# A hybrid attention and recurrence layer: head pairs projected earlier, half of an output projection inside the last pair, query swaps on GpSimd

## The chip, the cores and the metric

The kernel runs on one core of a Trainium2 chip. The metric is the device time of one execution in microseconds (us). Its engines are TensorE (PE; PEld are its weight loads), VectorE (DVE), ScalarE (ACT), GpSimd (POOL) and SyncE (SP), whose queue issues all DMA transfers of this kernel. TensorE's clock is granted at 2.4 or at 1.2 GHz; the profile gives the mean grant of a stretch as a share of the higher one.

## The reference, cut to what matters

One layer on 1024 frames of width 1024, with 16 learned frames in front (L = 1040):

```
u    = rms_norm(h);  proj = u @ w_in
       -> fq, fk, fv (8 heads x 64), ff (8), hq, hf, hi, hg (4 heads x 128)
fox  = per head: softmax(q.k/8 + c_t - c_s, causal) @ v,  c = cumsum(log_sigmoid(ff + bias))
hgrn = S_t = diag(f_t) S_{t-1} + k_t v_t^T,  o_t = S_t^T q_t;  rms_norm(o) * silu(hg)
h    = h + concat(fox, hgrn) @ w_out
h    = h + (silu(u2 @ w_gate) * (u2 @ w_up)) @ w_down,   u2 = rms_norm(h)
out  = rms_norm(h)[16:]
```

All is float32. The kernel splits each operand of a product into a high and a low part and forms three products (`mm3`: high x high, high x low, low x high), so that every product of the formulas is three on TensorE. A split is a cast on ScalarE (high part, L135) and a subtraction on VectorE or GpSimd (low part, L136).

## The kernel before, in words

The stages, in the order of the program: norm and transposition of the input (u, high and low, in `uT`); the recurrence heads (`hgrn_proj`, `hgrn_compute`), the values of the attention heads (`fox_v`) and their gates between them; the attention by pairs of heads (`fox_proj`, `fox_compute`); the output projection by tiles of 128 frames (`out_proj`) with the second norm; the FFN, in 22 blocks, by a scheme that saves products; the last product with `w_ffn_down` and the final norm. The change touches the attention and the start of the output projection, from about 345 to 600 us of the span.

**Projection of a pair** (`fox_proj`, L488). Weights for the keys and the queries of two heads are loaded and split (`load_m`; from pair 1 on GpSimd makes the low part, w_lo). `keys(i)` forms a third of the 1040 keys, `queries(i)` a half of the 1024 queries, each with 24 products into one of three `dense` PSUM banks; ScalarE evacuates the high part and VectorE the low part, into KS (keys) and QA (queries) of each head: one head dimension of 64 partitions holds the high part, the other 64 the low part. KS and QA come from pool `fxk0` for pairs 0 and 2, `fxk1` for 1 and 3, one buffer each: a pair can write them once the pair before last is done. `keys(0)` and `queries(0)` are traced before the pair's attention; `keys(1)` behind its group 0; `keys(2)` and `queries(1)` behind its group 1 (`rest`).

**Attention of a pair** (`fox_compute`, L604) runs over 4 groups g of 256 queries, and in each over its 2 heads (`fox_group`, L529). Group g needs keys up to 16 + 256(g + 1) and queries 256g to 256(g + 1). QB holds the same queries as QA with the halves of 64 partitions swapped; it is made by two transfers within SBUF (L532, L533). The scores are QA x KS and QB x KS (L546, L547) in PSUM bank `g`; VectorE adds the gate sums nl (or the masked block dm that GpSimd makes of them, L540) and takes the minimum (L552); ScalarE forms the exponential (L557); TensorE transposes it (L577), ScalarE and VectorE split it into PH and PL (L581, L582), TensorE multiplies it with v (L587), and the result goes through `mixp` to `mix_dram` (L598, L599, L616, L617). At the start of a pair `fox_head_load` loads v and nl (a row of 1040 broadcast to 128 partitions) and VectorE takes 4 columns of nl as tg (L524); GpSimd shifts nl by tg after each group (L602). v and nl have one buffer for each of the two heads, QB two.

**Output projection.** `out_proj(t)` (L687) loads the 8 blocks of `mix_dram` for its tile in three parts (4 to 7 are the recurrence heads, 0 to 3 the attention pairs), splits them into mh and ml (one buffer each), and forms 8 x 3 products for each half of 512 columns, the last pair's block at the end. Its weights are w_out in 8 blocks, cast and split into `woh` and `wol` by `load_wo` (L651): four blocks behind group 1 of pair 3, four behind its group 2, into space that is free once u is no longer read (`uT_pool` closes in `after_group(1)`).

**What sets the order.** The program is traced in the order of the Python code, and the framework's planner then sets the order on each engine: going through modelled time, it gives each engine, of the instructions whose inputs and buffers it takes to be ready, the one traced first. Each engine and SyncE's queue then keep that order on the chip and wait in it. So an instruction that is traced later can be run earlier, where an engine would have nothing else to do.

Of the kernel before, what the change touches and what calls it, by code (L numbers as in the profile page):

```python
# [49 lines left out]
def hybrid_trunk(  # L50
# [437 lines left out]
    def fox_proj(p, fxk):  # L488
        KS = [fxk.tile([P, L], F32R, name=f"KS{j}", tag=f"KS{j}") for j in range(2)]
        QA = [fxk.tile([P, SEQ], F32R, name=f"QA{j}", tag=f"QA{j}") for j in range(2)]  # L490
        wk, wq = (load_m(c + p * P, w_in[0], pool if p else None) for c in (C_FK, C_FQ))
        lanes = [(0, slice(0, 64), slice(64, 128)), (1, slice(64, 128), slice(0, 64))]

        def keys(i):
            c0, n = FULL[i]
            o = form1(u, wk, c0, n)
            for j, a, b in lanes:
                act.copy(KS[j][a, c0:c0 + n], o[a])
                vec.tensor_sub(KS[j][b, c0:c0 + n], o[a], f32(KS[j][a, c0:c0 + n]))

        def queries(i):
            c0, n = REAL[i]
            o = form1(u, wq, c0, n)
            q = slice(c0 - META, c0 - META + n)
            for j, a, b in lanes:
                act.activation(QA[j][a, q], o[a], AF.Copy, scale=-0.125)
                vec.scalar_tensor_tensor(QA[j][b, q], o[a], -0.125, f32(QA[j][a, q]), ALU.mult, ALU.subtract)

        keys(0)
        queries(0)  # L510
        rest = ((lambda: keys(1)), (lambda: (keys(2), queries(1))))
        return KS, QA, rest

    def fox_head_load(p, j):
        h = 2 * p + j
        vt = fx.tile([P, NT + 1, P], F32R, name=f"v{j}", tag=f"v{j}", bufs=1)
        sync.dma_start(out=f32(vt[:, :NT, :]), in_=v_dram[:NT, :, h, :].rearrange("t p c -> p t c"))
        pool.memset(f32(vt[:, NT, :]), 0.0)
        for r0 in (0, 32):
            sync.dma_start(out=f32(vt[r0:r0 + META, NT, :]), in_=v_dram[NT, :META, h, :])  # L520
        nl = fx.tile([P, L], F32, name=f"nl{j}", tag=f"nl{j}", bufs=1)
        sync.dma_start(out=nl, in_=nl_dram[h, :].partition_broadcast(P))
        tg = fx.tile([P, 4], F32, name=f"tg{j}", tag=f"tg{j}", bufs=2)
        vec.tensor_scalar(tg[:, 0:4], nl[:, META + 255::256], -1.0, None, ALU.mult)  # L524
        return vt, nl, tg
# [3 lines left out]
    def fox_group(p, j, g, KS, QA, vt, nl, tg, rr, t):  # L529
        QB = fx.tile([P, 256], F32R, name="QB", tag="QB")  # L530
        qc = 256 * g
        sync.dma_start(out=f32(QB[0:64]), in_=f32(QA[64:128, qc:qc + 256]))  # L532
        sync.dma_start(out=f32(QB[64:128]), in_=f32(QA[0:64, qc:qc + 256]))  # L533
        rs = small.tile([P, 2], F32, name="rs", tag="rs")
        Ss = []
        for ii in range(2):
            i = 2 * g + ii
            n = META + P * (i + 1)
            dm = fx.tile([P, P], F32, name="dm", tag="dm")
            pool.affine_select(out=dm, in_=nl[:, n - P:n], pattern=[[-1, P]], compare_op=ALU.is_ge, fill=BIG, base=0, channel_multiplier=1)  # L540
            S = fx.tile([P, L], F32, name="S_", tag="S_", bufs=4)
            mx = small.tile([P, 4], F32, name="mx", tag="mx")
            c0, prev, m = 0, 3e38, 0
            for w in CHUNKS[n]:
                sc = bank("g")
                pe.matmul(sc[:, :w], lhsT=QA[:, P * i:P * (i + 1)], rhs=KS[:, c0:c0 + w], start=True, stop=False)  # L546
                pe.matmul(sc[:, :w], lhsT=QB[:, P * ii:P * (ii + 1)], rhs=KS[:, c0:c0 + w], start=False, stop=True)  # L547
                e = min(c0 + w, n - P)
                for a, b, bias in ((c0, e, nl[:, c0:e]), (n - P, n, dm)):
                    if b > c0 + w:  # L550
                        continue
                    vec.tensor_tensor_reduce(out=S[:, a:b], in0=sc[:, a - c0:b - c0], in1=bias, scale=1.0, scalar=prev,  # L552
                                             op0=ALU.add, op1=ALU.min, accum_out=mx[:, m:m + 1])
                    prev = mx[:, m:m + 1]
                    m += 1
                c0 += w
            act.activation(S[:, :n], S[:, :n], AF.Exp, scale=-1.0, bias=prev, accum_out=rs[:, ii:ii + 1])  # L557
            Ss.append(S)
        vec.reciprocal(rr[:, :, j], rs)
        ob = bank("o", 1)  # L560

        def pv_meta():
            pt = bank("tr")
            for ii in range(2):
                pe.transpose(pt[:META, ii * P:(ii + 1) * P], Ss[ii][:, 0:META], ident)
            m = mzs[(j + g) % 2]
            act.copy(m[0:META], pt[:META, :256])
            return ((NT, m, 0),), vec.tensor_sub(m[32:48], pt[:META, :256], f32(m[0:META]))

        def pv_pair(b):  # L570
            pt = bank("tr")
            blks = ((256, 2 * b), (0, 2 * b + 1))
            for o, blk in blks:
                for ii in range(2):
                    if blk <= 2 * g + ii:
                        c = META + blk * P
                        pe.transpose(pt[:, o + ii * P:o + (ii + 1) * P], Ss[ii][:, c:c + P], ident)  # L577
            hi = fx.tile([P, 512], F32R, name="PH", tag="PH", bufs=3)
            lo = fx.tile([P, 512], F32R, name="PL", tag="PL", bufs=3)
            s0 = 0 if b < g else P  # L580
            act.copy(hi[:, s0:], pt[:, s0:])  # L581
            last = vec.tensor_sub(lo[:, s0:], pt[:, s0:], f32(hi[:, s0:]))  # L582
            return [(blk, t[:, o:o + 256], P if blk > 2 * g else 0) for o, blk in blks for t in (hi, lo)], last

        def pv_mm(parts, _, late):
            for i, (blk, r, q0) in enumerate(parts):
                m = pe.matmul(ob[:, q0:256], lhsT=vt[:, blk, :], rhs=r[:, q0:256], start=blk == NT, stop=blk == 2 * g + 1 and i == 3)  # L587
                if i == 0 and late is not None:
                    after(m, late)

        pend = pv_meta()
        for b in range(g + 1):
            nxt = pv_pair(b)
            pv_mm(*pend, nxt[-1])
            pend = nxt
        pv_mm(*pend, None)
        tj = t[j * HD:(j + 1) * HD]
        act.copy(tj, ob[HD:P, :256])  # L598
        vec.tensor_add(tj, tj, ob[0:HD, :256])  # L599
        if g < 3:  # L600
            w = META + 256 * (g + 1)
            pool.tensor_scalar(nl[:, :w], nl[:, :w], 1.0, tg[:, g:g + 1], ALU.mult, ALU.add)  # L602

    def fox_compute(p, KS, QA, rest, extra=None):  # L604
        heads = [fox_head_load(p, j) for j in range(2)]
        for g in range(4):
            mixp = fx.tile([P, 256], F32, name="mixp", tag="mixp")
# [7 lines left out]
                pe.transpose(rb[:, ii * P:(ii + 1) * P], rw[:, ii, :], ident)  # L615
            vec.tensor_mul(mixp, mixp, rb[:, :256])  # L616
            sync.dma_start(out=mix_dram[p, :, 256 * g:256 * (g + 1)], in_=mixp)  # L617
            if g < 2:
                rest[g]()
            if extra:  # L620
                extra(g)
    a = hgrn_proj(0)
# [17 lines left out]
    for t in mzs:  # L640
        pool.memset(f32(t), 0.0)
    for s in range(3):
        if s:
            b = fox_proj(s, (fxk0, fxk1)[s % 2])
        fox_compute(s, *b)
    fxk0_pool.__exit__(None, None, None)
    b = fox_proj(3, fxk1)
    op_pool, wo_pool = left("op", 2), left("wo")
    wos, op, wo = {}, None, None

    def load_wo(ks):  # L651
        for k in ks:
# [4 lines left out]
            split(hi, lo, st)  # L657
            wos[k] = (hi, lo)

    def after_group(g):  # L660
        nonlocal op, wo
        if g == 1:
            uT_pool.__exit__(None, None, None)
            op, wo = op_pool.__enter__(), wo_pool.__enter__()
        load_wo(((), WO1, WO2, ())[g])

    fox_compute(3, *b, after_group)
    fxk1_pool.__exit__(None, None, None)
# [18 lines left out]
    def out_proj(t):  # L687
# [1 line left out]
        mt = op.tile([P, KT, P], F32, name="mt", tag="mt", bufs=1)  # L689
        mh = op.tile([P, KT, P], F32R, name="mh", tag="mh", bufs=1)  # L690
        ml = op.tile([P, KT, P], F32R, name="ml", tag="ml", bufs=1)
        for a, b in ((4, 8), (0, 3), (3, 4)):
            sync.dma_start(out=mt[:, a:b, :], in_=mix_dram[a:b, :, ts_].rearrange("k p c -> p k c"))
            split(mh[:, a:b, :], ml[:, a:b, :], mt[:, a:b, :])
        ht = op.tile([P, D], F32, name="ht", tag="ht")
        sync.dma_start(out=ht, in_=x[0, ts_, :])
        os_ = (dense(), dense())
        order = (4, 5, 6, 7, 0, 1, 2, 3)
        for ks in (order[:7], order[7:]):
            for half in range(2):  # L700
                hs = slice(512 * half, 512 * half + 512)
                for k in ks:
                    mm3(os_[half], mh[:, k, :], ml[:, k, :], wos[k][0][:, hs], wos[k][1][:, hs], k == 4, k == 3)
        for half in range(2):
            hs = slice(512 * half, 512 * half + 512)
            vec.tensor_add(ht[:, hs], ht[:, hs], os_[half])
        sync.dma_start(out=h_dram[t], in_=ht)
        return ht

# [439 lines left out]
```

## Time and profile before

| | |
|---|---|
| median of 3 runs | 1327.34 us (1324.17 to 1333.28) |
| profiled execution | 1328.32 us, its span 1326.2 us |
| granted TensorE clock over the span | 0.988 |
| busy: PE, PEld, DVE, ACT, POOL | 1283.4, 1074.1, 909.7, 619.6, 98.1 us |

The profile is of one execution. Times count from the start of its span. A busy time is the sum of an engine's instruction times; those of PE overlap, as products are pipelined, so idle PE is read from what is not busy, and from the waits. "x<-y" names the tile written and those read.

### The profile page before, as it was taken

Reading aid. Unit: us, or ns where it says so; the run is one execution under the profiler, and the core shown is the slowest. Engines: PE = TensorE matmul, PEld = TensorE weight load, DVE = VectorE, ACT = ScalarE, POOL = GpSimd, SP = SyncE. Lnnn points to the kernel's source line nnn. Section 1 sums busy time; section 2 is a strip of 40 time slices with the busy share of each in tenths; the row PEclk is TensorE's granted clock in tenths of the full one; section 3 lists DMA queues with packets and bytes.
Section 4 is the critical chain, followed back from the end, with each engine's and each line's share of the span. In section 5 each row is a group of like instructions: output and inputs, shape, how many; then the busy total and the mean of one; then the engine's idle time right before and its main releaser. Section 6 shows DMA issues by size and latency. Waiting matters only on the chain.

```text
span 1326.2 us, 18596 instructions
## 1 busy us (share of the span) xinstructions
PE 1283.4 (97%) x6577; PEld 1074.1 (81%) x6577; DVE 909.7 (69%) x1876; ACT 619.6 (47%) x1328; POOL 98.1 (7%) x190
## 2 busy tenths in 40 slices
PE   8999999999999999799989999999999999999997
PEld 6888898988878878688868888888888888888886
DVE  6458566665578878776788666666766664597777
ACT  6347555564566656554453333333233233433464
POOL 0130101010142231100000000000000000000000
PEclk9999999999999999799999999999999999999999
DMA  7231212121323323443413334324323335955352
GB/s 247 82 105 41 75 41 88 41 77 52 106 71 103 87 71 89 142 145 112 142 50 107 99 111 130 109 88 135 103 89 110 119 119 206 335 182 165 107 174 85
DMA packets 140253, 150.58 MB, mean 114 GB/s; under 512 B 7944, under 2 KB 100424, under 8 KB 140160
## 3 DMA queue, kind: packets, MB, share of 16 engines
q1 hardware_dynamic: 140160, 149.39, 35.1%
q8 instruction: 52, 0.85, 0.3%
q14 instruction: 41, 0.34, 0.1%
HBM read 105.98 MB, written 39.19 MB: 109 GB/s over the span
## 4 chain that ended last, share of the span: by engine, by line
PE 78%; DVE 9%; DMA 5%; ACT 5%; issue 2%; POOL 1%; SPq 0%; ACTq 0%; POOLq 0%; DVEq 0%
PE pb L167 10%; PE pb L168 10%; PE pb L169 10%; PE dense L169 8%; PE dense L168 7%; PE dense L167 7%; PE g L168 4%; PE g L167 4%; PE g L169 4%; PE o L587 2%; PE tr L577 2%; PE g L546 1%; DMA nl<-nl_dram 1%; PE g L547 1%; DMA QB<-QA 1%
## 5 line engine op out<-in xcount | busy, mean ns | idle before, releaser
L167 PE MATMUL dense<-u_hi,w_hi 128*128 128x512 f32 (+2 forms) x384 | 142.1, 370 | 0.0
L168 PE MATMUL dense<-u_lo,w_hi 128*128 128x512 f32 (+2 forms) x384 | 141.6, 369 | 0.0
L169 PE MATMUL dense<-u_hi,w_lo 128*128 128x512 f32 (+2 forms) x384 | 141.6, 369 | 0.0
L167 PE MATMUL pb<-T_hi,bh 128*128 128x512 f32 x352 | 138.5, 393 | 3.0 <-ACT bh L135 3.0
L168 PE MATMUL pb<-T_lo,bh 128*128 128x512 f32 x352 | 138.3, 393 | 0.6 <-DVE T_lo L136 0.6
L169 PE MATMUL pb<-T_hi,bl 128*128 128x512 f32 x352 | 137.9, 392 | 0.1
L135 ACT CAST bh<-sS 128x512 fp32r<-128x512 f32 x88 | 54.5, 621 | 159.6 <-PE pb L168 78.5
L135 ACT CAST h_hi<-h_st 128x1024 fp32r<-128x1024 f32 (+1 forms) x43 | 41.8, 971 | 85.6 <-PE o L168 38.4
L167 PEld LDWEIGHTS pb<-T_hi,bh 128*128 128x128 f32 x352 | 66.5, 189 | 18.5 <-ACT bh L135 3.4
L169 PEld LDWEIGHTS pb<-T_hi,bl 128*128 128x128 f32 x352 | 66.5, 189 | 14.9 <-DVE bl L136 0.4
L168 PEld LDWEIGHTS pb<-T_lo,bh 128*128 128x128 f32 x352 | 66.4, 189 | 14.9 <-DVE T_lo L136 1.0
L169 PEld LDWEIGHTS dense<-u_hi,w_lo 128*128 128x128 f32 x384 | 73.6, 192 | 5.9
L168 PEld LDWEIGHTS dense<-u_lo,w_hi 128*128 128x128 f32 x384 | 73.2, 191 | 6.4
L167 PEld LDWEIGHTS dense<-u_hi,w_hi 128*128 128x128 f32 x384 | 73.1, 190 | 6.4
L169 PE MATMUL pb<-w_hi,h_lo 128*128 128x512 f32 x198 | 77.6, 392 | 0.0
L168 PE MATMUL pb<-w_lo,h_hi 128*128 128x512 f32 x198 | 77.5, 391 | 0.0
L167 PE MATMUL pb<-w_hi,h_hi 128*128 128x512 f32 x198 | 77.1, 389 | 0.0
L136 DVE TENSOR_TENSOR w_lo<-w_st,w_hi 128x1024 fp32r<-128x1024 f32 (+1 forms) x41 | 49.6, 1209 | 30.9 <-ACT w_hi L135 30.9
L136 DVE TENSOR_TENSOR h_lo<-h_st,h_hi 128x1024 fp32r<-128x1024 f32 (+1 forms) x43 | 48.3, 1123 | 31.6 <-ACT h_hi L135 31.2
L167 PE MATMUL g<-B_hi,w_hi 128*128 128x512 f32 x168 | 66.5, 396 | 1.0 <-ACT p L814 1.0
L168 PE MATMUL g<-B_lo,w_hi 128*128 128x512 f32 x168 | 67.0, 399 | 0.0
L169 PE MATMUL g<-B_hi,w_lo 128*128 128x512 f32 x168 | 65.8, 392 | 0.0
(839 smaller groups left out, 3315.8 us busy)
## 6 DMA issues: line engine op xcount, KB each, us to landing
w_st<-in_w_in_dram SPq DMA_DIRECT2D x24, 512.0 KB, 3.9
w_st<-in_w_ffn_gate_dram SPq DMA_DIRECT2D x22, 512.0 KB, 3.8
w_st<-in_w_ffn_up_dram SPq DMA_DIRECT2D x22, 512.0 KB, 3.9
B<-in_w_ffn_down_dram SPq DMA_DIRECT2D x20, 512.0 KB, 6.2
h_st<-S SPq DMA_DIRECT2D x20, 512.0 KB, 4.0
h_st<-A SPq DMA_DIRECT2D x15, 512.0 KB, 4.5
A<-g SPq DMA_DIRECT2D x22, 256.0 KB, 2.0
S<-u SPq DMA_DIRECT2D x22, 256.0 KB, 3.7
```

Of the source, the lines that this page charges most:

```text
L135: later(act.copy(hi, src))
L136: return later((engine or vec).tensor_sub(lo, src, f32(hi)))
L167: pe.matmul(o, lhsT=ah, rhs=bh, start=first, stop=False, skip_group_check=skip)
L168: pe.matmul(o, lhsT=ah, rhs=bl, start=False, stop=False, skip_group_check=skip)
L169: pe.matmul(o, lhsT=al, rhs=bh, start=False, stop=last, skip_group_check=skip)
L546: pe.matmul(sc[:, :w], lhsT=QA[:, P * i:P * (i + 1)], rhs=KS[:, c0:c0 + w], start=True, stop=False)
L547: pe.matmul(sc[:, :w], lhsT=QB[:, P * ii:P * (ii + 1)], rhs=KS[:, c0:c0 + w], start=False, stop=True)
L577: pe.transpose(pt[:, o + ii * P:o + (ii + 1) * P], Ss[ii][:, c:c + P], ident)
L587: m = pe.matmul(ob[:, q0:256], lhsT=vt[:, blk, :], rhs=r[:, q0:256], start=blk == NT, stop=blk == 2 * g + 1 and i == 3)
```

## The change

The projection of a pair is traced as a whole: pair 0's before the attention starts, and pair s + 1's behind the attention of pair s. nl gets two buffers for each head. QB is written by two GpSimd copies in place of two transfers. The space of u closes before pair 3's attention; w_out's blocks are loaded behind its groups 0 and 1. Behind group 1, `out_half` forms, for the first two tiles of the output projection, the four recurrence blocks' share, and keeps it in SBUF (tag h2, two buffers); `out_proj` of these tiles forms the other four blocks only and adds that half.

```diff
         keys(0)
         queries(0)
-        rest = ((lambda: keys(1)), (lambda: (keys(2), queries(1))))
-        return KS, QA, rest
+        keys(1)
+        keys(2)
+        queries(1)
+        return KS, QA
...
-        nl = fx.tile([P, L], F32, name=f"nl{j}", tag=f"nl{j}", bufs=1)
+        nl = fx.tile([P, L], F32, name=f"nl{j}", tag=f"nl{j}", bufs=2)
...
-        sync.dma_start(out=f32(QB[0:64]), in_=f32(QA[64:128, qc:qc + 256]))
-        sync.dma_start(out=f32(QB[64:128]), in_=f32(QA[0:64, qc:qc + 256]))
+        pool.tensor_copy(QB[0:64], QA[64:128, qc:qc + 256])
+        pool.tensor_copy(QB[64:128], QA[0:64, qc:qc + 256])
...
-            if g < 2:
-                rest[g]()
...
     for s in range(3):
-        if s:
-            b = fox_proj(s, (fxk0, fxk1)[s % 2])
         fox_compute(s, *b)
+        b = fox_proj(s + 1, (fxk0, fxk1)[(s + 1) % 2])
     fxk0_pool.__exit__(None, None, None)
-    b = fox_proj(3, fxk1)
+    uT_pool.__exit__(None, None, None)
...
+    def out_half(ts):
+        mt, mh, ml = (op.tile([P, KT, P], d, name=n_, tag=n_, bufs=1) for n_, d in (("mt", F32), ("mh", F32R), ("ml", F32R)))
+        for i, t in enumerate(ts):
+            a = slice(4 * i, 4 * i + 4)
+            sync.dma_start(out=mt[:, a, :], in_=mix_dram[4:8, :, t * P:(t + 1) * P].rearrange("k p c -> p k c"))
+            split(mh[:, a, :], ml[:, a, :], mt[:, a, :])
+        for i, t in enumerate(ts):
+            halves[t] = op.tile([P, D], F32, name="h2", tag="h2")
+            for hs in (slice(0, 512), slice(512, 1024)):
+                o = dense()
+                for k in range(4):
+                    j = 4 * i + k
+                    mm3(o, mh[:, j, :], ml[:, j, :], wos[4 + k][0][:, hs], wos[4 + k][1][:, hs], k == 0, k == 3)
+                act.copy(halves[t][:, hs], o)
...
     def after_group(g):
-        nonlocal op, wo
+        if g < 2:
+            load_wo((WO1, WO2)[g])
         if g == 1:
-            uT_pool.__exit__(None, None, None)
-            op, wo = op_pool.__enter__(), wo_pool.__enter__()
-        load_wo(((), WO1, WO2, ())[g])
+            out_half(ORDER[:2])
...
-        for a, b in ((4, 8), (0, 3), (3, 4)):
+        for a, b in ((4, 8), (0, 3), (3, 4))[0 if half is None else 1:]:
...
-        order = (4, 5, 6, 7, 0, 1, 2, 3)
+        order = (4, 5, 6, 7, 0, 1, 2, 3) if half is None else (0, 1, 2, 3)
...
+        if half is not None:
+            vec.tensor_add(ht, ht, half)
```

## Rows read from the trace of the kernel before

**Rows 1.** The page's first part: busy time of each engine, its share of the span, and the number of its instructions.

```profile
PE 1283.4 (97%) x6577; PEld 1074.1 (81%) x6577; DVE 909.7 (69%) x1876; ACT 619.6 (47%) x1328; POOL 98.1 (7%) x190
```

**Rows 2.** The windows view from 345 to 700 us. Columns: the stretch and its length; busy time (and number of instructions) of PE, PEld, DVE, ACT, POOL; granted clock; DMA share; GB/s.

```profile
345.00:376.00 31.00, 28.92 (x159) 25.58 (x158) 13.28 (x47) 12.50 (x37) 6.17 (x14) 0.94 0.40 112
376.00:470.00 94.00, 89.53 (x596) 77.18 (x594) 80.00 (x279) 64.37 (x147) 28.47 (x59) 1.00 0.32 91
470.00:520.00 50.00, 46.75 (x297) 40.58 (x297) 38.36 (x133) 30.64 (x69) 11.33 (x24) 0.97 0.31 84
520.00:560.00 40.00, 32.98 (x177) 26.51 (x176) 29.68 (x90) 22.92 (x49) 8.41 (x17) 0.83 0.36 115
560.00:596.00 36.00, 34.78 (x208) 29.55 (x207) 27.70 (x72) 20.54 (x44) 1.67 (x6) 1.00 0.50 157
596.00:700.00 104.00, 98.25 (x445) 78.17 (x444) 74.94 (x155) 47.76 (x112) 0.00 (x0) 0.98 0.30 102
```

**Rows 3.** SyncE's timeline at the stores that end group 3 of pairs 0 to 3. Columns: start, duration, engine, line, operation, names.

```profile
421.74 0.34 SPq L617 DMA_DIRECT2D mix_dram<-mixp  x1
...
470.64 0.34 SPq L617 DMA_DIRECT2D mix_dram<-mixp  x1
...
524.68 0.35 SPq L617 DMA_DIRECT2D mix_dram<-mixp  x1
...
592.75 0.32 SPq L617 DMA_DIRECT2D mix_dram<-mixp  x1
```

**Rows 4.** TensorE's timeline (matrix products) around 366, 486 and 543 us; in brackets the idle time before an instruction and what ended it.

```profile
365.43 0.32 PE L167 MATMUL dense<-u_hi,w_hi 128*128 128x346 f32 x1
367.74 0.49 PE L547 MATMUL g<-KS,QB 128*128 128x256 f32 x2 [1.99 <-DMA QB<-QA]
...
486.19 0.57 PE L547 MATMUL g<-KS,QB 128*128 128x328 f32 x2 [1.73 <-DMA QB<-QA]
...
541.33 0.40 PE L168 MATMUL dense<-u_lo,w_hi 128*128 128x512 f32 x1
541.56 0.39 PE L169 MATMUL dense<-u_hi,w_lo 128*128 128x512 f32 x1
543.35 0.57 PE L546 MATMUL g<-KS,QA 128*128 128x328 f32 x2 [1.40 <-DVE QA L507]
546.15 0.89 PE L547 MATMUL g<-KS,QB 128*128 128x328 f32 x2 [2.23 <-DMA QB<-QA]
```

**Rows 5.** ScalarE's timeline at the evacuation of the last half of the queries of a pair: one head each of pairs 1, 2 and 3.

```profile
393.73 0.57 ACT L506 ACTIVATE QA<-dense 64x512 fp32r<-64x512 f32 x1
...
481.08 0.59 ACT L506 ACTIVATE QA<-dense 64x512 fp32r<-64x512 f32 x1
...
543.54 0.59 ACT L506 ACTIVATE QA<-dense 64x512 fp32r<-64x512 f32 x1
```

**Rows 6.** The waits of TensorE from 345 to 596 us: who waited for what, total, times, longest.

```profile
PE g L547 <- DMA QB<-QA: 6.0, 3, 2.2
...
PE g L546 <- DVE QA L507: 1.4, 1, 1.4
```

**Rows 7.** Transfers into nl and QB (number, KB of one, median from issue to landing); VectorE's tg (minimum, median and maximum ns, first and last start), its idle time before it (us, times), and its first one on the timeline.

```profile
nl<-nl_dram SPq DMA_DIRECT2D x8, 520.0 KB, 4.5
...
QB<-QA SPq DMA_DIRECT2D x64, 64.0 KB, 2.0
...
L524 DVE TENSOR_SCALAR tg<-nl x8: 163/170/2194, 362.2 to 518.6; 128x4 f32<-128x4 f32 x8
...
  DMA nl<-nl_dram: 11.0, 5
...
362.23 0.17 DVE L524 TENSOR_SCALAR tg<-nl 128x4 f32<-128x4 f32 x1 [5.35 <-DMA nl<-nl_dram]
```

**Rows 8.** GpSimd's groups of instructions by shape (count | busy us, mean ns | idle before), and its splits of projection weights from 368 to 596 us (minimum, median and maximum ns, first and last start).

```profile
L540 POOL TENSOR_SCALAR_AFFINE_SELECT dm<-nl 128x128 f32<-128x128 f32 x64 | 19.5, 308 | 107.6 <-DVE mx L552 86.5 <-DMA nl<-nl_dram 17.9 <-DVE rr L559 3.1
...
L236 POOL CAST uf_hi<-u_hi 128x1024 fp32r<-128x1024 f32 x4 | 4.4, 1108 | 50.6 <-ACT u_hi L151 50.6
...
L612 POOL COPY rw<-rr 128x256 f32<-128x256 f32 x16 | 6.3, 397 | 19.5 <-DVE rr L559 7.6 <-PE dense L169 6.7 <-PE tr L565 3.1
...
L136 POOL TENSOR_TENSOR w_lo<-w_st,w_hi x4: 2390/2394/2409, 376.3 to 478.8; 128x1024 fp32r<-128x1024 f32 x4
```

**Rows 9.** GpSimd's and VectorE's timelines around 454.5 us.

```profile
454.47 2.39 POOL L136 TENSOR_TENSOR w_lo<-w_st,w_hi 128x1024 fp32r<-128x1024 f32 x1 [3.81 <-ACT w_hi L135]
...
454.20 0.57 DVE L552 CUSTOM_DVE_ANT_0 S__5155<-g,nl,mx 128x346 f32<-128x346 f32 x1
454.70 2.19 DVE L524 TENSOR_SCALAR tg<-nl 128x4 f32<-128x4 f32 x1
```

**Rows 10.** w_out: VectorE's splits and ScalarE's casts (minimum, median and maximum ns, first and last start), ScalarE's idle time before the casts (us, times), the longest of these on its timeline, and the loads.

```profile
L136 DVE TENSOR_TENSOR wol<-w_st,woh x8: 1212/1226/1743, 543.5 to 570.0; 128x1024 fp32r<-128x1024 f32 x8
...
L135 ACT CAST woh<-w_st x8: 1032/1046/1053, 542.5 to 569.0; 128x1024 fp32r<-128x1024 f32 x8
...
  DMA w_st<-in_w_out_dram: 6.0, 4
...
548.99 1.04 ACT L135 CAST woh<-w_st 128x1024 fp32r<-128x1024 f32 x1 [3.78 <-DMA w_st<-in_w_out_dram]
...
w_st<-in_w_out_dram SPq DMA_DIRECT2D x8, 512.0 KB, 4.5
```

More of the change, by code (lines that the diff above doesn't have):

```diff
@@ L602, in fox_group, with fox_compute @@
             pool.tensor_scalar(nl[:, :w], nl[:, :w], 1.0, tg[:, g:g + 1], ALU.mult, ALU.add)
-    def fox_compute(p, KS, QA, rest, extra=None):
+    def fox_compute(p, KS, QA, extra=None):
         heads = [fox_head_load(p, j) for j in range(2)]
@@ L642, in hybrid_trunk @@
     for s in range(3):
-        if s:
-            b = fox_proj(s, (fxk0, fxk1)[s % 2])
         fox_compute(s, *b)
+        b = fox_proj(s + 1, (fxk0, fxk1)[(s + 1) % 2])
     fxk0_pool.__exit__(None, None, None)
-    b = fox_proj(3, fxk1)
+    uT_pool.__exit__(None, None, None)
     op_pool, wo_pool = left("op", 2), left("wo")
-    wos, op, wo = {}, None, None
+    op, wo = op_pool.__enter__(), wo_pool.__enter__()
+    wos = {}
     def load_wo(ks):
@@ L658, in load_wo @@
             wos[k] = (hi, lo)
+    halves = {}
+    def out_half(ts):
[12 more added lines that the diff above has]
+                act.copy(halves[t][:, hs], o)
     def after_group(g):
-        nonlocal op, wo
+        if g < 2:
+            load_wo((WO1, WO2)[g])
         if g == 1:
-            uT_pool.__exit__(None, None, None)
-            op, wo = op_pool.__enter__(), wo_pool.__enter__()
-        load_wo(((), WO1, WO2, ())[g])
+            out_half(ORDER[:2])
     fox_compute(3, *b, after_group)
@@ L691, in out_proj @@
         ml = op.tile([P, KT, P], F32R, name="ml", tag="ml", bufs=1)
-        for a, b in ((4, 8), (0, 3), (3, 4)):
+        half = halves.pop(t, None)
+        for a, b in ((4, 8), (0, 3), (3, 4))[0 if half is None else 1:]:
             sync.dma_start(out=mt[:, a:b, :], in_=mix_dram[a:b, :, ts_].rearrange("k p c -> p k c"))
@@ L697, in out_proj @@
         os_ = (dense(), dense())
-        order = (4, 5, 6, 7, 0, 1, 2, 3)
-        for ks in (order[:7], order[7:]):
-            for half in range(2):
-                hs = slice(512 * half, 512 * half + 512)
+        order = (4, 5, 6, 7, 0, 1, 2, 3) if half is None else (0, 1, 2, 3)
+        for ks in (order[:-1], order[-1:]):
+            for i in range(2):
+                hs = slice(512 * i, 512 * i + 512)
                 for k in ks:
[L703 to L706, printed above, removed]
+                    mm3(os_[i], mh[:, k, :], ml[:, k, :], wos[k][0][:, hs], wos[k][1][:, hs], k == order[0], k == 3)
+        if half is not None:
+            vec.tensor_add(ht, ht, half)
+        for i in range(2):
+            hs = slice(512 * i, 512 * i + 512)
+            vec.tensor_add(ht[:, hs], ht[:, hs], os_[i])
         sync.dma_start(out=h_dram[t], in_=ht)
```

## The prediction

> **What bounds the kernel now.** Page first: TensorE is busy 97% of the span [rows 1], so time can only be won where it idles or runs at the lower clock. The windows view over the attention stage and what follows [rows 2] says where that is. Window less PE busy gives idle of 2.1, 4.5, 3.2, 7.0 and 1.2 us in the five stretches from 345 to 596, 18.0 us in all; from 596 to 700 it is another 5.8 us. The granted clock stands under 1.00 in three of the five: (1 - clock) x length is 1.9, 1.5 and 6.8 us of full-speed time, 10.2 us in all. **28.2 us is therefore the whole prize** in the stage the change touches, 2.1% of the kernel. VectorE is not far behind TensorE there: 80.0 of 94 us between 376 and 470.
>
> Next the stores that end each group of 256 queries, on SyncE's queue [rows 3]. The last group of the four head pairs ends at 421.7, 470.6, 524.7 and 592.8: pairs 1 and 2 (counting from 0) take 49 and 54 us, pair 3 takes 68.
>
> Then TensorE's own timeline around three of its longest holes [rows 4]. Two end with the transfer QB<-QA (1.99 and 1.73 us idle). The third has two parts: 1.40 us until VectorE has written the second half of pair 3's queries, then 2.23 us until QB<-QA lands. In the three stretches of [rows 2] that hold one, and only there within the stage, part of the time was granted at the lower of the two levels (1.2 GHz). ScalarE's timeline [rows 5] says why the second and third are late: pair 1's last queries were evacuated at 393.7, while pair 0 was running, but pair 2's at 481.1, inside pair 2, and pair 3's at 543.5, inside pair 3, where group 2 needs them. The waits of TensorE over the stage [rows 6] put a total on it: 6.0 us for QB<-QA and 1.4 us for the queries.
>
> **The change part by part.**
>
> *Whole projection before its pair.* Nothing is added: 24 products for each third of the keys and half of the queries, in both kernels. The planner takes the earliest traced instruction that it holds ready, so keys 1, keys 2 and queries 1 of a pair, until now traced behind groups 0 and 1 of that pair, come ahead of them, and of the other pool's KS and QA they only need that the pair before last is finished. The hole at 541.56 to 546.15 has no cause left (3.6 us idle), nor that at 484 (1.7 us). Half of the clock stretch behind them should go too.
>
> *GpSimd copies for QB.* Removed: 64 issues on SyncE and a landing of 2.0 us in the median [rows 7], in front of every group's second product. Added: 64 GpSimd copies of 64x256. No row has that form; a copy of 128x256 takes 0.40 us and a cast of 128x1024 1.11 [rows 8], so 0.40 each is nearest, with 0.31 (the 128x128 select) as lower and 1.11 as upper bound. 64 x 0.40 = 26 us, beside the 49.9 us that GpSimd is busy of the 220 from 376 to 596 [rows 2]. In time they are hidden; in latency two copies (0.8 us) replace a landing. In front of a copy stands its wait for QA and for a free QB. Behind it in GpSimd's queue stand the masks dm, the nl update and rw, for which VectorE and TensorE wait; ahead of it can stand the low part of a projection weight, 2.4 us [rows 8], four times after 376. QB has two buffers, one group of lead, so I charge +2 us (0 to 4 x 2.4 = +9.6).
>
> *Two nl buffers.* The nl loads (520 KB, 4.5 us) no longer wait for the pair before. VectorE stood 11.0 us before tg for them, 5 times [rows 7], part of it with TensorE fed. One tg itself took 2.19 us instead of 0.17, behind a GpSimd split [rows 9]; that stays. At the start of pair 0 nothing changes for nl: its tg ran at 362.2, and the first product with QB only at 367.7 [rows 4, 7].
>
> *Half of the output projection, two tiles.* 2 x 2 x 4 x 3 = 48 products at 0.23 us (neighbouring starts, [rows 4]) = 11.0 us move into pair 3 from behind it, where TensorE is full anyway: no gain in themselves, only filler for holes. The transfers of mix are the same, earlier. Added: 4 ScalarE evacuations of 512 columns, nearest QA's at 0.59 [rows 5] = 2.4 us, and 2 VectorE additions of 128x1024, nearest the split of that size at 1.23 [rows 10] = 2.5 us. They run beside products; +1.5 us (0 to +4.8).
>
> *Output weights one group earlier.* 8 loads, 8 casts of 1.05 on ScalarE, 8 splits of 1.23 on VectorE [rows 10], unchanged in number. ScalarE stood 6.0 us before them waiting for loads, and what is behind them in its queue stood with it. Traced earlier than groups 1 to 3, they can do that again: +1 us (0 to +24, below).
>
> **The sum, by stretch of [rows 2].** 345 to 376: 2.1 idle + 1.9 clock, take -3.0, as TensorE had fill until 365.4 and nl was there at 362.2. 376 to 470: -1.5 of 4.5, since the remaining waits are short ones for VectorE. 470 to 520: -3.0 of 4.7. 520 to 560: 13.8 are there; the 3.6 direct and 4.9 of the clock's 6.8, as TensorE was not always what others waited for: -8.5. 560 to 596: -0.5. That is -16.5, plus 4.5 of costs: **-12 us**. The profiled execution took 1328.3 us (span 1326.2), 1.0 above the median of 1327.34; 1328.3 - 12 = **1316 us**, 0.9% under that median.
>
> GpSimd and VectorE can hold each other up. With a GpSimd split from 454.47, tg took 2.19 us, while the score reduction that began at 454.20 (one operand from PSUM, one from SBUF) kept its 0.57 [rows 9]. One wol split took 1.74 against a median of 1.23 [rows 10]. So I charge 0 for the copies beside score work. The Trainium skill, SBUF — State Buffer, section "Who interferes with whom", speaks against the copies in part: VectorE with two SBUF inputs, or in a two-port mode, and a GpSimd instruction that reads SBUF exclude each other for a whole instruction. By that rule VectorE would pay for the copies of pair 3, where its two-input splits run, and the sum would be that of the port rival below.
>
> **The rivals.**
>
> *All of it goes.* Every hole and fall closes, with 2 us of costs: 1328.3 - 28.2 + 2 = 1302 us. For it: holes and falls come in a chain, and one early projection breaks it. Against it: VectorE was busy 85% of 376 to 470.
>
> *Projected ahead already.* Pair 1's were [rows 5]; the planner filled holes from the lowest place too. Then pairs 0 to 2 only win the waits themselves, and pair 3 turns from waiting for queries to waiting for VectorE: -(7.4 + 1.9 + 1.5) + 4.5 = -6.3, 1322 us. The change would then not do what it says for most pairs.
>
> *The port.* Each of the 16 copies of pair 3 meets a two-input split and holds VectorE for 0.40: +6.4, so 1323 us. The rule of the Trainium skill's page SBUF — State Buffer would give that. As for its weight, the trace bears it out for tg, not for the reduction beside it [rows 9], and TensorE would have to be waiting for VectorE each time.
>
> *Output weights hold ScalarE (slower).* The casts woh take places ahead of groups 1 to 3; if all eight wait as long as the longest did (3.78 us, [rows 10]), they stop ScalarE 30.2 us, 24.2 more than now, with the exponentials and P casts queued behind and no filler for TensorE, as the half projection needs the same weights; one more clock fall like that in 470 to 520 is 1.5. 1328.3 - 12 + 24.2 + 1.5 = 1342 us. It decides when a load is issued less than its landing (4.5 us) ahead of its cast, eight times. For it: two w_st buffers only. Against: only four of eight waited so far, and the space is free earlier.
>
> **Chances and range.** Forecast (1309 to 1322) 0.36, all of it 0.21, ahead already 0.24, the port 0.08, slower 0.11. A measurement of this kernel (runs 1324.2 to 1333.3) tells about 1% from no change: under 1314.1 is faster, over 1340.6 slower. Faster: all of it 0.21 and 0.17 of the forecast's own part, 0.38. Slower: 0.10. The rest, 0.52, is within 1%. The range 1301 to 1331 leaves out the slower rival (0.11) and some 0.06 under 1301; it takes in GpSimd's upper bound (1316 + 7.6) and that of the evacuations.
>
> **What the profile after would show.** Projection right: all ScalarE evacuations of QA for pair 3 before its first group ends, and pair 3 from 68 down to some 55 us. Copies right: no wait of TensorE for QB over 0.5 us, GpSimd busy some 26 us longer. Clock right: the attention stage at or near 1.00. Two nl buffers right: no idle of VectorE before tg. I am wrong upwards if TensorE's waits turn to GpSimd copies, or ScalarE stands before woh; wrong downwards if idle in 376 to 596 falls under 8 us.

## The result, and the profile after

The changed kernel takes 1316.27 us in the median (1315.78 to 1319.01, 7 runs) beside 1327.34 us for the kernel before: a ratio of 0.9914, 95% interval 0.9894 to 0.9934. A second comparison on another occasion gave 0.9935 (0.9918 to 0.9952). It is faster, by 0.9 and 0.65% in the two comparisons, and so inside the 1% that the prediction counts as no clear change; the forecast was 1316.

The page's first part and the windows view of the kernel after, with the columns of [rows 1, 2]:

```profile
PE 1277.7 (97%) x6577; PEld 1068.3 (81%) x6577; DVE 910.1 (69%) x1878; ACT 621.2 (47%) x1332; POOL 125.2 (10%) x254
```

```profile
345.00:376.00 31.00, 28.78 (x162) 25.06 (x162) 15.98 (x65) 14.94 (x45) 13.41 (x32) 0.94 0.43 134
376.00:470.00 94.00, 92.53 (x607) 80.24 (x607) 75.69 (x259) 62.53 (x138) 35.09 (x74) 1.00 0.25 74
470.00:520.00 50.00, 48.97 (x323) 42.73 (x322) 40.41 (x131) 31.54 (x72) 16.94 (x42) 1.00 0.12 37
520.00:560.00 40.00, 33.44 (x179) 26.15 (x178) 32.77 (x89) 25.50 (x55) 14.01 (x27) 1.00 0.56 180
560.00:596.00 36.00, 35.33 (x213) 28.87 (x212) 28.21 (x84) 22.31 (x51) 3.66 (x9) 1.00 0.28 88
596.00:700.00 104.00, 98.22 (x450) 78.50 (x449) 79.01 (x161) 49.17 (x110) 0.00 (x0) 1.00 0.30 96
```

By the measure of the prediction (length less PE busy, plus (1 - clock) x length) the five stretches from 345 to 596 now lose 4.1, 1.5, 1.0, 6.6 and 0.7 us: 13.8 in place of 28.2. Two of the three clock falls in the stage are gone. GpSimd is busy 27.1 us longer (125.2 against 98.1). The whole span gives a second account, in which overlapping products count once: TensorE's busy time falls by 5.7 us (1283.4 to 1277.7, the same 6577 products) and its idle time, span less busy, by 6.0 us (42.8 to 36.8). Together that is the 11.7 us by which the span is shorter (1326.2 to 1314.5).

The stores that end pairs 0 to 3 (L619 here, as in [rows 3]), one head of pair 3's last queries on ScalarE, and one product in three (L167) of the output projection from 500 us to the last attention product, at 587 after and, the last row, at 591 before (minimum, median and maximum ns, first and last start):

```profile
413.12 0.37 SPq L619 DMA_DIRECT2D mix_dram<-mixp  x1
...
459.80 1.00 SPq L619 DMA_DIRECT2D mix_dram<-mixp  x1
...
518.71 0.74 SPq L619 DMA_DIRECT2D mix_dram<-mixp  x1
...
589.12 0.32 SPq L619 DMA_DIRECT2D mix_dram<-mixp  x1
```

```profile
526.11 0.59 ACT L506 ACTIVATE QA<-dense 64x512 fp32r<-64x512 f32 x1
```

```profile
L167 PE MATMUL dense<-woh,mh x31: 387/395/505, 530.2 to 585.4; 128*128 128x512 f32 x31
```

```profile
L167 PE MATMUL dense<-woh,mh x21: 387/397/793, 555.8 to 590.1; 128*128 128x512 f32 x21
```

Pair 0 ends 8.6 us earlier than in [rows 3], pair 1 10.8, pair 2 6.0, pair 3 only 3.6: pair 3 takes 70.4 us (518.71 to 589.12) where it took 68.1. But about 31 x 3 products of the output projection are done by its end, 21 x 3 in the kernel before. The 30 products between them are 30 x 0.23 = 6.9 us [rows 4], and 3.6 + 6.9 makes 10.5 of the 11.7 us by which the span is shorter. **Of these 10.5 us, 6.0 were won by the end of pair 2 and some 4.5 in pair 3; in pair 3 they show as output products done, not as an earlier end.** The measure above divides it much the same way: up to 520 us 6.6 us less are lost, from 520 to 596 us 7.8 us.

### The profile page after: what moved, and what is told of

It reads as the page before. It is cut to its first block, busy times and chain, and to the rows that moved or that the text cites. A ratio compares the mean times of both kernels' runs of the same rounds, so it can differ in the third digit from the quotient of the medians.

```text
span 1314.5 us, 18565 instructions
## 1 busy us (share of the span) xinstructions
PE 1277.7 (97%) x6577; PEld 1068.3 (81%) x6577; DVE 910.1 (69%) x1878; ACT 621.2 (47%) x1332; POOL 125.2 (10%) x254
## 4 chain that ended last, share of the span: by engine, by line
PE 79%; DVE 10%; ACT 5%; DMA 3%; issue 2%; POOL 2%; SPq 0%; POOLq 0%; ACTq 0%; DVEq 0%
PE pb L167 11%; PE pb L168 11%; PE pb L169 10%; PE dense L169 8%; PE dense L168 7%; PE dense L167 7%; PE g L168 4%; PE g L167 4%; PE g L169 4%; PE o L589 2%; PE tr L579 2%; PE g L548 1%; PE g L549 1%; DMA w_st<-in_w_out_dram 1%; PE g L422 1%
## 5 line engine op out<-in xcount | busy, mean ns | idle before, releaser
L167 PE MATMUL dense<-u_hi,w_hi 128*128 128x512 f32 (+2 forms) x384 | 141.7, 369 | 0.0
L167 PE MATMUL pb<-T_hi,bh 128*128 128x512 f32 x352 | 137.8, 391 | 3.0 <-ACT bh L135 3.0
L167 PEld LDWEIGHTS pb<-T_hi,bh 128*128 128x128 f32 x352 | 66.1, 188 | 18.4 <-ACT bh L135 3.4
L167 PEld LDWEIGHTS dense<-u_hi,w_hi 128*128 128x128 f32 x384 | 73.0, 190 | 6.8
L167 PE MATMUL pb<-w_hi,h_hi 128*128 128x512 f32 x198 | 77.1, 389 | 0.0
L167 PE MATMUL g<-B_hi,w_hi 128*128 128x512 f32 x168 | 66.5, 396 | 1.4 <-ACT p L833 1.4
```

What stands on the lines that cost most here:

```text
L167: pe.matmul(o, lhsT=ah, rhs=bh, start=first, stop=False, skip_group_check=skip)
```

## The experiments

Each ratio is to the kernel before, run on the same occasion, with its 95% interval. "Lost" is the measure above, summed over 345 to 596 us of the profiled execution; the kernel before has 28.2. The medians come from several occasions: beside a_dma to d_nl1 the kernel before took 1324.3 us, beside after_again, e_copy, i_qb4 and h_dummy 1325.9, beside the last four 1324.7, and at the forecast 1327.3. So a range that was stated in us is up to 3 us too high there, and the ratios decide.

| kernel | median us | ratio | lost us |
|---|---|---|---|
| after, first and second time | 1316.3, 1316.7 | 0.9914, 0.9935 | 13.8, 11.2 |
| a_dma: after, QB by transfers | 1322.4 | 0.9980 (0.9972 to 0.9989) | 20.9 |
| b_rest: after, old projection order | 1315.9 | 0.9929 (0.9915 to 0.9943) | 12.3 |
| c_nohalf: after, no half projection | 1315.2 | 0.9922 (0.9908 to 0.9937) | 9.9 |
| d_nl1: after, one nl buffer | 1317.7 | 0.9944 (0.9931 to 0.9958) | 12.4 |
| e_copy: before, QB by copies | 1316.9 | 0.9935 (0.9921 to 0.9950) | 16.3 |
| f_proj: before, new projection order | 1318.6 | 0.9951 (0.9932 to 0.9971) | 16.3 |
| i_qb4: before, four QB buffers | 1319.7 | 0.9953 (0.9940 to 0.9965) | 20.1 |
| h_dummy: e_copy, transfers kept idle | 1323.2 | 0.9981 (0.9972 to 0.9990) | 23.2 |
| m_poolq: before, transfers by GpSimd | 1326.5 | 1.0016 (1.0001 to 1.0031) | 27.7 |
| best1 | 1320.8 | 0.9970 (0.9957 to 0.9984) | 18.5 |
| best2 | 1313.5 | 0.9909 (0.9889 to 0.9930) | 12.8 |

### One part undone at a time

**a_dma.**

```diff
-        pool.tensor_copy(QB[0:64], QA[64:128, qc:qc + 256])
-        pool.tensor_copy(QB[64:128], QA[0:64, qc:qc + 256])
+        sync.dma_start(out=f32(QB[0:64]), in_=f32(QA[64:128, qc:qc + 256]))
+        sync.dma_start(out=f32(QB[64:128]), in_=f32(QA[0:64, qc:qc + 256]))
```

> The changed kernel with one part undone: QB by the two transfers again. Theory (the copies take a 2.0 us landing out of each group, and with it holes and clock falls): slower than the changed kernel by 4 to 7 us, 1320 to 1323 us, with waits of TensorE for QB<-QA back at over 3 us in total. Rival (once the whole projection comes before its pair, QA is there early and the transfer is hidden): within 2 us of 1316 us and no wait for QB over 1 us after the first group.

1322.4 us: of the gain only 0.2% of the time is left. TensorE's wait for QB and the windows row from 520 to 560 us:

```profile
PE g L549 <- DMA QB<-QA: 1.8, 1, 1.8
```

```profile
520.00:560.00 40.00, 32.95 (x156) 26.59 (x155) 27.69 (x72) 23.45 (x48) 8.68 (x14) 0.87 0.57 180
```

The time lies in the theory's range in us; by the ratios it is 6 to 9 us slower than the kernel after, where 4 to 7 were expected. The reason is not the theory's: the direct wait is 1.8 us, once. What came back are holes in pair 3 with a lower clock (12.3 us lost from 520 to 560 us, 6.6 in the kernel after).

**b_rest** puts `keys(1)`, and `keys(2)` with `queries(1)`, behind groups 0 and 1 of their pair again, through `rest`, and with them the closing of u and `load_wo`:

```diff
+        rest = ((lambda: keys(1)), (lambda: (keys(2), queries(1))))
...
         if g == 1:
+            uT_pool.__exit__(None, None, None)
+            op, wo = op_pool.__enter__(), wo_pool.__enter__()
+        load_wo(((), WO1, WO2, ())[g])
```

> The changed kernel with the projection traced in the old order again (second and last third of the keys and second half of the queries behind groups 0 and 1 of their pair), and with it the space of u closed and w_out loaded one group later, as before; copies, two nl buffers and the half output projection stay. Theory (late queries of pairs 2 and 3 make the holes at group 2): 1322 to 1326 us, with a hole of over 1.5 us and a clock fall in pair 3. Rival (the copies do it, the planner fills from below either way): 1316 to 1319 us.

1315.9 us, the rival's time. The late queries of pair 3 are back, with the same wait as in [rows 6], and cost nothing that can be measured beside the copies:

```profile
PE g L546 <- DVE QA L507: 1.4, 1, 1.4
```

**c_nohalf** drops one call:

```diff
-        if g == 1:
-            out_half(ORDER[:2])
```

> The changed kernel without the half output projection of two tiles; out_proj forms all eight blocks of every tile. Theory (filler only, other filler takes its place): 1315 to 1319 us. Rival (without this filler TensorE runs empty in groups 2 and 3 of pair 3 and its clock falls): 1321 to 1326 us, fewer output products done when the last attention product runs, and a granted clock under 0.95 between 520 and 560 us.

1315.2 us, the theory: no gain from the half projection is to be seen. The clock from 520 to 560 us is 0.96, and that stretch loses 5.7 us, no more than with it:

```profile
520.00:560.00 40.00, 35.95 (x189) 27.60 (x188) 32.83 (x97) 26.83 (x59) 17.68 (x30) 0.96 0.59 188
```

**d_nl1.**

```diff
-        nl = fx.tile([P, L], F32, name=f"nl{j}", tag=f"nl{j}", bufs=2)
+        nl = fx.tile([P, L], F32, name=f"nl{j}", tag=f"nl{j}", bufs=1)
```

> The changed kernel with one nl buffer for each head, as before. Theory: VectorE stands before tg again at the start of pairs 1 to 3, some 4 us in all, of which TensorE has filler for most: 1317 to 1320 us. Rival (the nl buffers are what joins the pairs): 1321 us or more, with holes of TensorE at the three changes of pair.

1317.7 us, in the theory's range, but its interval meets that of the kernel after: an effect of the second nl buffer is not shown.

### One part alone

**after_again** is the changed kernel unaltered.

> The changed kernel once more, beside the three that follow. Every theory: a ratio to the kernel before of 0.990 to 0.994.

It gave 0.9935. Its first stretch and the one in pair 3:

```profile
345.00:376.00 31.00, 29.56 (x175) 25.14 (x174) 17.85 (x71) 15.93 (x48) 13.80 (x33) 1.00 0.42 134
520.00:560.00 40.00, 35.05 (x184) 27.55 (x182) 34.01 (x94) 26.10 (x54) 14.39 (x28) 0.96 0.56 178
```

The clock fall before 376 of the first execution is absent here (1.4 us idle in the stretch, 2.2 there), and one in pair 3 is there (5.0 us idle, 6.6 in the first execution at 1.00). So executions of one kernel differ in such falls, and a fall in one profile is not by itself the mark of a change.

**e_copy** is the kernel before with the two `pool.tensor_copy` lines in place of the two transfers, and nothing else.

> The kernel before with one part of the change alone: QB by two GpSimd copies. Theory now (the copies carry nearly the whole gain; the projection order, the nl buffers and the half output projection add at most 2 us together): ratio to the kernel before 0.991 to 0.995. Rival (each part is enough to free the copies' or the projection's gain only together with another): ratio 0.996 to 1.000.

0.9935, as the theory had it, and the same as the whole change beside it. Its windows:

```profile
345.00:376.00 31.00, 29.16 (x171) 24.94 (x172) 17.61 (x70) 16.30 (x49) 13.82 (x33) 1.00 0.33 100
376.00:470.00 94.00, 92.68 (x626) 81.64 (x625) 81.59 (x287) 65.30 (x150) 39.18 (x87) 1.00 0.25 75
470.00:520.00 50.00, 48.31 (x310) 42.21 (x308) 37.48 (x124) 29.66 (x66) 16.65 (x40) 0.97 0.20 62
520.00:560.00 40.00, 35.09 (x191) 28.68 (x190) 30.89 (x83) 25.29 (x49) 14.95 (x23) 0.91 0.50 152
560.00:596.00 36.00, 34.60 (x190) 28.24 (x189) 24.71 (x70) 18.20 (x44) 0.95 (x3) 1.00 0.33 110
```

Against [rows 2] it saves in each of the first four stretches: 2.1, 3.2, 1.6 and 5.3 us; of the first, 1.9 us is a clock fall that the kernel after shows in one execution and not in the other.

**f_proj** is the kernel before with the new order alone (the hunks on `keys(1)`, `rest` and the loop over pairs).

> The kernel before with the projection order of the change alone (each pair's whole projection traced before that pair's attention); QB by transfers, one nl buffer, w_out as before. Theory (copies carry the gain): ratio to the kernel before 0.997 to 1.003. Rival (the order alone takes the late queries of pair 3 out, 3.6 us of hole and half of a clock fall): ratio 0.992 to 0.996.

0.9951: here the rival was right. So either part alone frees most of the gain, and the two do not add up. a_dma has this order, and beside it two nl buffers, the early w_out and the half projection; its ratio of 0.9980 is worse than 0.9951. So beside transfers those other parts together cost some 0.3%. Its wait for QB, and its first output product:

```profile
PE g L549 <- DMA QB<-QA: 1.8, 1, 1.8
```

```profile
533.68 0.78 PE L167 MATMUL dense<-woh,mh 128*128 128x512 f32 x1
```

The wait is down from 6.0 to 1.8 us, although the transfers are all there: with whole projections in front, QA is early. And the first output product runs at 533.7, 22 us earlier than before; the load of `mt` that it needs goes out at 527.2, though the transfers stand in SyncE's queue, since the last product that reads u, whose space `mt` takes, starts at 525.1 here and at 541.6 in the kernel before [rows 4].

### What the transfers cost: the landing, or the queue

**i_qb4.**

```diff
-        QB = fx.tile([P, 256], F32R, name="QB", tag="QB")
+        QB = fx.tile([P, 256], F32R, name="QB", tag="QB", bufs=4)
```

> The kernel before with four QB buffers in place of two, still filled by transfers, so that a transfer can be issued two groups earlier. Theory (what counts is the landing where queries come late, at the start of pair 0 and at group 2 of pairs 2 and 3, which no buffer shortens): ratio 0.997 to 1.001. Rival (SyncE's queue standing for a free QB is what delays the transfers and what is behind them): ratio 0.991 to 0.995.

0.9953, just outside the rival's range (0.991 to 0.995) and far from the theory's. SyncE's wait for a free QB, first in the kernel before, then with four buffers (total us, times, longest), and its windows rows from 345 to 560 us:

```profile
SPq L532 <- PE g L547: 46.8, 16, 7.0
```

```profile
SPq L532 <- PE g L547: 23.6, 12, 4.9
```

```profile
345.00:376.00 31.00, 28.73 (x158) 25.50 (x157) 12.54 (x47) 11.73 (x35) 5.93 (x14) 0.94 0.45 128
376.00:470.00 94.00, 92.80 (x622) 79.78 (x622) 82.36 (x294) 66.67 (x156) 29.07 (x61) 1.00 0.32 91
470.00:520.00 50.00, 49.35 (x326) 43.16 (x325) 40.65 (x138) 32.34 (x72) 12.43 (x27) 1.00 0.32 93
520.00:560.00 40.00, 32.95 (x169) 25.68 (x169) 30.34 (x84) 23.90 (x50) 9.73 (x15) 0.83 0.47 140
```

Standing half as long, SyncE's queue gives back 4.1 us from 470 to 520 and 3.3 from 376 to 470, and nothing in pair 3 (13.9), which needs something else. (At the start of pair 0 4.1 us are lost, as before; 1.9 of them are the clock fall that comes and goes.)

**h_dummy** keeps e_copy's copies and issues the two transfers as well, into a tile QD that nothing reads:

```diff
+        QD = fx.tile([P, 256], F32, name="QD", tag="QD")
+        sync.dma_start(out=QD[0:64], in_=f32(QA[64:128, qc:qc + 256]))
+        sync.dma_start(out=QD[64:128], in_=f32(QA[0:64, qc:qc + 256]))
```

> The kernel before with QB by GpSimd copies, and with the two transfers kept, into a tile that nothing reads: SyncE issues and the DMA engines move as much as before, but no product waits for a landing. Theory (latency): within 2 us of the kernel with the copies alone. Rival (the copies win by freeing SyncE's queue and the DMA engines): 5 us or more slower than it, near the kernel before.

1323.2 us, 6.3 more than e_copy: the rival again. No product waits for these transfers; they only stand in SyncE's queue and move their bytes. But one product waits 2.1 us for a load of v, a wait that e_copy doesn't have. The first load of `mt` for the output projection, on SyncE, and the first output product, in the kernel before, in e_copy, and in h_dummy; in the last two with the last product that reads u ahead of them:

```profile
551.25 1.18 SPq L693 DMA_DIRECT2D mt<-mix_dram  x2
...
555.81 0.79 PE L167 MATMUL dense<-woh,mh 128*128 128x512 f32 x1 [0.69 <-ACT mh L135]
```

```profile
533.75 0.39 PE L169 MATMUL dense<-u_hi,w_lo 128*128 128x512 f32 x1
...
534.55 0.43 SPq L693 DMA_DIRECT2D mt<-mix_dram  x1
...
539.91 0.80 PE L167 MATMUL dense<-woh,mh 128*128 128x512 f32 x1 [3.35 <-ACT mh L135]
```

```profile
535.79 0.39 PE L169 MATMUL dense<-u_hi,w_lo 128*128 128x512 f32 x1
...
543.25 0.58 SPq L696 DMA_DIRECT2D mt<-mix_dram  x1
...
549.27 0.78 PE L167 MATMUL dense<-woh,mh 128*128 128x512 f32 x1
```

The load goes out at 551.3, 534.6 and 543.3, which is 9.7, 0.8 and 7.5 us after the last product that reads u (541.56 in the kernel before [rows 4]); the first output product runs at 555.8, 539.9 and 549.3. In pair 3 TensorE has no other filler once the last queries are projected, so a late load leaves the hole open. (The planner's order differs a little between these kernels too, and h_dummy moves the bytes as well. i_qb4 moves the same bytes as the kernel before and gains 6.2 us, so bytes alone are not the cost; how queue and bytes share the 6.3 us is not shown.)

**m_poolq** is the kernel before with `pool.dma_start` in place of `sync.dma_start` for QB.

> The kernel before with the same two transfers for QB, issued from GpSimd's queue in place of SyncE's. Theory now (SyncE's queue stands for a free QB, 47 us in all, and holds nl, v, w_out and the stores behind it): ratio to the kernel before 0.993 to 0.997, waits for QB<-QA still there. Rival (the landing itself is what costs): ratio 0.998 or more, with waits of TensorE for QB<-QA of 5 us or more.

1.0016: no gain, the rival's time. TensorE's wait for QB, and GpSimd's issue of one of the two transfers (minimum, median and maximum ns):

```profile
PE g L547 <- DMA QB<-QA: 13.8, 4, 5.6
```

```profile
L532 POOL DMA_DIRECT2D QB<-QA x32: 516/554/728, 354.5 to 561.1; - x32
```

SyncE's queue is free of them here, but the wait for QB grew from 6.0 to 13.8 us; the longest, 5.6 us, ends with transfers issued from 543 to 547 us, which landed after 5.3 to 5.8 us against a median of 2.0 [rows 7]. And each issue takes GpSimd 0.55 us. So the landing does count where it is long; this run can't say how queue and landing share the gain.

### Two attempts at a better version

Both leave out the half projection and load nl ahead of v. **best1** loads w_out one group later, as the kernel before did; **best2** loads it early and has four QB buffers.

```diff
-        sync.dma_start(out=f32(vt[:, :NT, :]), in_=v_dram[:NT, :, h, :].rearrange("t p c -> p t c"))
...
         sync.dma_start(out=nl, in_=nl_dram[h, :].partition_broadcast(P))
+        sync.dma_start(out=f32(vt[:, :NT, :]), in_=v_dram[:NT, :, h, :].rearrange("t p c -> p t c"))
```

> An attempt at a better version: the changed kernel without the half output projection, w_out loaded behind groups 1 and 2 as before, and nl loaded ahead of v. Theory (pair 0 can start some 3 us earlier, since nl is what its first reductions wait for, and the holes around w_out in group 0 of pair 3 go): 1310 to 1314 us. Rival (TensorE has filler there and is full): 1314 to 1317 us.

> Another: the changed kernel without the half output projection, w_out early, nl loaded ahead of v, and four QB buffers filled by the copies. Theory: 1311 to 1315 us. Rival (QB is no longer waited for, more buffers bring nothing): as the other attempt or slower.

best1 took 1320.8 us, worse than both had it; best2 1313.5, in the theory's range, ratio 0.9909. Output products (one in three) from 500 us to each one's last attention product at 577 and 584 us, and best1's stretch in pair 3:

```profile
L167 PE MATMUL dense<-woh,mh x10: 387/394/518, 530.1 to 574.7; 128*128 128x512 f32 x10
```

```profile
L167 PE MATMUL dense<-woh,mh x28: 387/397/775, 529.2 to 582.7; 128*128 128x512 f32 x28
```

```profile
520.00:560.00 40.00, 29.39 (x163) 22.92 (x162) 34.85 (x109) 28.72 (x61) 17.45 (x34) 0.91 0.53 165
```

best1 ends its attention earliest of all, with 10 x 3 output products done and 10.6 us idle in pair 3; best2 has 28 x 3. They differ in two things, w_out's loads and QB's buffers, but neither is what the trace shows missing: the loads of w_out go out from 529.4 to 547.3 and from 528.1 to 546.2, and no product waits for QB in either. What is late in best1 is the low part ml of the first mix tile, on VectorE, first best1, then best2:

```profile
556.62 0.68 DVE L136 TENSOR_TENSOR ml<-mt,mh 128x512 fp32r<-128x512 f32 x1
```

```profile
533.83 0.69 DVE L136 TENSOR_TENSOR ml<-mt,mh 128x512 fp32r<-128x512 f32 x1
```

In best1 the high part mh was cast from 527.4, so ml stood 29 us in VectorE's order behind attention work. Which of the two edits led the planner to that order is open. best2's interval overlaps that of the kernel after, so it is not shown to be better; it is as fast, without the half projection.

## Why the prediction was right, and where not

**The sum was right, its parts were not, and that it came to 1316 is in part luck:** the gain by stretch was put 2 us too high, and the costs of 4.5 us did not show. Forecast by stretch were -3.0, -1.5, -3.0, -8.5 and -0.5 us, -16.5 in all; by the same measure the profile shows +0.1, -3.0, -3.7, -7.3 and -0.6, -14.4. The first failed. The prediction counted on fill until 365.4 and on nl at 362.2; with the whole projection traced first the fill ended at 361.0, nl came at 362.1 as before, and the hole is as long as it was. It now ends with VectorE, whose first reductions need nl:

```profile
363.11 0.36 PE L548 MATMUL g<-KS,QA 128*128 128x256 f32 x1 [2.12 <-DVE mx L554]
```

The second was sized at half of what it gave. A further 2.1 us came from behind the stage, where 596 to 700 had clock 0.98 and has 1.00 in this execution; c_nohalf and a_dma show 0.98 there, e_copy and i_qb4 1.00, so it is not shown to be the change's. Set against 11.7 us of span the measure overstates, and it does so in its clock part: from 345 to 700 us that part falls by 10.4 us, while TensorE's busy time over the whole span fell by 5.7. The idle part, 6.1 us from 345 to 596, agrees with the 6.0 of the span.

**The costs (+4.5) were mis-sized.** No wait of TensorE for a GpSimd copy appears after; b_rest and e_copy have one of 1.4 to 1.5 us. The copy itself was as estimated, 0.39 us for 0.40, in the kernel after:

```profile
L534 POOL CAST QB<-QA x32: 392/393/398, 354.0 to 561.5; 64x256 fp32r<-64x256 f32 x32
L535 POOL CAST QB<-QA x32: 391/396/405, 354.5 to 561.9; 64x256 fp32r<-64x256 f32 x32
```

(Minimum, median and maximum ns, first and last start.) In e_copy a copy that began beside a split of w_out on VectorE took 1.45 us, and the split its usual 1.22: here GpSimd was held up, and not VectorE, as the port rival had it.

```profile
537.81 1.45 POOL L533 CAST QB<-QA 64x256 fp32r<-64x256 f32 x1 [0.53 <-DVE QA L507]
...
537.78 1.22 DVE L136 TENSOR_TENSOR wol<-w_st,woh 128x1024 fp32r<-128x1024 f32 x1
```

The half projection's 1.5 us is not to be seen (c_nohalf). For w_out ScalarE stood 3.3 us, less than the 6.0 of [rows 10], so the slower rival fell by its own test.

**The step that failed is the first part**, "whole projection before its pair", with "pair 3 from 68 down to some 55 us". The late queries did go (526.1 against 543.5), the 3.6 us of hole with them, but pair 3 takes 70.4 us in place of the 55, and with the copies in place the order is worth nothing that can be measured (b_rest). I gave the holes to the waits that ended them. Those waits were real, but what decided was whether TensorE had something else ready meanwhile: in pair 3, output products. These waited for loads that SyncE's queue issued late beside the QB transfers (the kernel before, h_dummy), or, where the load of `mt` was early (526.4 in a_dma, 527.2 in f_proj, 522.6 in best1), for ml, which came late in VectorE's order (542.3, 542.6 and 556.6, against 534.1 in the kernel after).

All fourteen traces fit this. Of the output products, counted one in three at L167, 13 to 16 had started by 550 us where 4.4 to 8.2 us were lost from 520 to 560 us (after, after_again, b_rest, c_nohalf, d_nl1, best2), 5 to 7 where it was 8.5 to 12.3 (a_dma, e_copy, f_proj), and 0 to 2 where it was 10.8 to 14.2 (before, i_qb4, h_dummy, m_poolq, best1). That is agreement, not proof: no run changes the filler alone.

**The copies were charged as a short latency and a cost**; by e_copy they alone bring as much as the whole change. The prediction removed 64 issues from SyncE and named no one behind them; it should have gone through nl, mt and w_out there one by one.

**Rivals.** "All of it goes" fell: 13.8 and 11.2 us remain lost. "Projected ahead already" said that the order brings little: true beside the copies, false alone (f_proj). The port fell by size. VectorE's tg and the w_out splits after (minimum, median and maximum ns, first and last start), and its commonest split from PSUM before and after (count, busy us, mean ns, idle before):

```profile
L526 DVE TENSOR_SCALAR tg<-nl x8: 152/170/211, 362.1 to 455.0; 128x4 f32<-128x4 f32 x8
```

```profile
L136 DVE TENSOR_TENSOR wol<-w_st,woh x8: 1220/1224/1401, 528.1 to 553.0; 128x1024 fp32r<-128x1024 f32 x8
```

```profile
L582 DVE TENSOR_TENSOR PL<-tr,PH 128x512 fp32r<-128x512 f32 x48 | 32.4, 688 | 3.2 <-ACT PH L581 2.4
```

```profile
L584 DVE TENSOR_TENSOR PL<-tr,PH 128x512 fp32r<-128x512 f32 x48 | 32.3, 687 | 4.1 <-ACT PH L583 3.0
```

The longest split is 1.40 us against 1.74 in [rows 10], the longest tg 0.21 against 2.19. The split with one operand in PSUM takes 687 ns in the mean in the kernel with GpSimd's copies and took 688 without. The trace so agrees with the Trainium skill, SBUF — State Buffer, section "Who interferes with whom", by which VectorE with at most one SBUF input, outside its two-port modes, doesn't contend with GpSimd.

## What to carry to other kernels

When a hole ends with a transfer, look also at what filler the busy engine lacked in it, and at what is queued behind that transfer: taking a transfer out of an in-order queue can be worth more to the loads behind it than to its reader (of the 9.0 us that the copies gained in e_copy, 6.3 were lost again when the transfers ran without a reader). Here two changes that each bring the same late filler forward did not add up, and one with the rest of the parts was slower than alone (a_dma against f_proj), so run each part alone before keeping the whole. Here two lines of the change do what all of it does.

## What was not expected of the hardware

The 64 transfers that nothing reads cost 6.3 us (h_dummy against e_copy) without any product waiting for them. A GpSimd copy of 64x256 that shifts 64 partitions took 0.39 us in the median, as much as one of 128x256 that shifts none [rows 8], and up to 1.45 beside a split with two SBUF inputs on VectorE (e_copy), while the issue of a transfer of the same size from GpSimd's queue occupied it for 0.55 us. The clock of one stretch, 345 to 376, was 0.94 and 1.00 in two executions of one kernel with 2.2 and 1.4 us of idle in it, 1.9 us by the measure; f_proj kept 1.00 there with 2.3 us idle.
